# A decoder layer: order of the inner norms, of the first query's weights and of the compression's last weights

## The chip, the cores and the metric

The kernel runs on one core of one Trainium2 chip, as one program. The metric is device time in microseconds: 1134.9 us, the median of three runs from 1133.58 to 1134.92. Times inside the program come from one profiled execution.

## The reference

One decoder layer on 512 tokens of width 1024, all in float32. Two half-step SwiGLU FFNs (hidden width 2816) stand around a token mixer; each of the three is normed before and after:

```python
h = rms_norm(x, ffn1_pre[l])
x = x + 0.5 * rms_norm(swiglu(h, ffn1_w_gate[l], ffn1_w_up[l], ffn1_w_down[l]), ffn1_post[l])
h = rms_norm(x, mix_pre[l])
y = token_mixer(h, w_in[l], nsa_pe_k[l], nsa_w_ck1[l], nsa_w_ck2[l], nsa_pe_v[l],
                nsa_w_cv1[l], nsa_w_cv2[l], w_nsa_o[l], w_dil_o[l], w_mix_out[l])
x = x + rms_norm(y, mix_post[l])
h = rms_norm(x, ffn2_pre[l])
x = x + 0.5 * rms_norm(swiglu(h, ffn2_w_gate[l], ffn2_w_up[l], ffn2_w_down[l]), ffn2_post[l])
```

The mixer projects `h` with `w_in` and runs two kinds of attention side by side. The first, sparse attention (NSA), has 8 query heads in 2 groups and three branches: compressed keys and values (overlapping blocks of 32 tokens, through a hidden layer of 256 with gelu), selected blocks, and a window. At this length every block is selected, so that the second and third branch are both plain causal attention. The other kind, dilated attention, has 12 heads in 3 groups. Gates merge the two, and `w_mix_out` closes the mixer.

## The kernel before

Every float32 operand of a matrix product is split into two parts that TensorE takes: `hi`, a cast on ScalarE (line 107), and `lo`, the rest, a subtraction on VectorE (line 108); `split` does both. A product is then three matmuls, `mm3`, lines 130 to 132. Weights arrive in `raw`, three buffers of 1 MB that SyncE's queue fills, and their parts go to `whi` and `wlo`, three tiles of 128x1024 each. A buffer that rotates is free again when its last reader is done. Matrix results lie in eight PSUM banks under four names: S (3), T (2), V (1), F (2).

The code is traced in the order written; a scheduler then orders each engine's instructions by readiness, and every engine runs its own list in order, waiting on semaphores. `issue_after(x)` tells the scheduler that what is traced inside goes behind instruction `x` on the same engine; it adds no wait for `x` to end.

The work runs in this order: the first FFN's gate and up products (a Strassen form for most of the width), its down product (`ffn_down`, to about 349 us), the NSA part of the mixer (`nsa`, about 349 to 530), dilated attention (`dil`), the merge and `w_mix_out` (`mixer` and `down`, to about 800), and the second FFN.

**The norms between the parts.** A tile t holds 128 tokens. At the end of `ffn_down`, and of `down`, each tile takes these steps: mean square of the result (`meansq`, ScalarE, line 139), root (`rstd`: VectorE line 148, then a power on GpSimd, line 152), a multiplication by the gain, the update of x (lines 640 and 273), and, for the next part's norm, two more squares, another root, the scaled rows `tmp` (line 198), eight transposes (line 203), casts into `xh` (line 206) and rests into `xl` (line 210). `finish` starts the next norm and leaves the last three steps as a function in `self.pending`, to be called between later matmuls. In `ffn_down` the last product, T4, has two halves, for tiles 2 and 3; `between` runs after the first half. In `down`, the last eight weights of the second column half are held as split tiles, and each tile t runs through them (line 264).

**The start of the mixer.** `positions` transposes a small tile of position rows into a bank T (line 754). `nsa` projects the keys, in between calls the pending transposes, then projects the values (`v_nsa`, `v_weights`) and splits the first half of the key compression's weights (`hidden_early`, into x_s). Then 16 heads follow (four query pairs, two groups, two branches), with probabilities two heads behind the scores. For the first head: `proj_T` projects the query pair from a `raw` of its own, and `q_parts` writes the query's parts (lines 715 to 718, tiles Q). `hb_scores` multiplies with the keys (lines 724 and 725, banks S); line 730 adds the masked distances (`W`, the distance matrix `dm` times the head's slope, line 1050) and takes the maximum; line 731 is the exponential. `hb_probs` scales by the gate over the sum (ScalarE line 969, GpSimd line 971), transposes (line 980) and splits into PT; `hb_values` multiplies with the values (line 995). Between the heads stand the compression: `hidden` (line 814), first for the keys and then for the values, with its last two weight blocks split through `whi` and `wlo`; `gelu`, `compressed`, the compressed scores `cmp_pair` (line 916); and, as filling, units of the merge gates (`merge_unit`: a projection into a bank F, a copy, line 1085). Tiles NN, three of 128x1024, hold token sums in the first FFN and later rows of the second FFN's down weights (`mixer_sums`).

Of the kernel before, what the change touches and what calls it, by code (L numbers as in the profile page):

```python
# [26 lines left out]
DFF = 2816  # L27
NF = DFF // P
MIX_TAIL = 8
BUSY = 4, 2, 5, 2, 4  # L30
GATES_AHEAD = 4
LAG = 2
# [28 lines left out]
class Layer:  # L61
# [166 lines left out]
    def down(self, acts, wload, nk, tail, tags, post, finish):  # L228

        nc = self.nc
        gain = None
        self.pending = []
        ms0, y0 = [], []
        for d in range(2):
            banks = [self.bank(tag) for tag in ("STFV", "STFS")[d]]
            held = []

            def mm(t, k, w):  # L240
                c = slice(t * P, (t + 1) * P)
                hi, lo = acts[k]
                self.mm3(banks[t], hi[:, c], lo[:, c], w[0], w[1], k == 0, k == nk - 1)

            for k0 in range(0, nk, 2):
                src = wload(d, k0)
                if d == 1 and k0 >= nk - tail:
                    for j in range(2):
                        w = [self.slot(tags.pop(0), F32R) for _ in range(2)]
                        self.split(w[0], w[1], src[:, j])  # L250
                        held.append((k0 + j, w))
                else:
                    hi, lo = self.wsplit(src, [2, S])
                    for j in range(2):
                        for t in range(NT):
                            mm(t, k0 + j, (hi[:, j], lo[:, j]))
            if d == 0:
                gain = post()
                for t in range(NT):
                    ms0.append(self.meansq(banks[t], S))  # L260
                    nc.vector.tensor_mul(banks[t], banks[t], gain[0][0])
                    y0.append(banks[t])
                continue
            for t in range(NT):
                for k, w in held:
                    mm(t, k, w)
                if t in (1, 2) and self.pending:
                    self.pending.pop(0)()
                r = self.rstd([ms0[t], self.meansq(banks[t], S)])
                y1 = self.slot("ring")  # L270
                nc.vector.tensor_mul(y1, banks[t], gain[0][1])
                for x, y in ((self.x[2 * t], y0[t]), (self.x[2 * t + 1], y1)):
                    nc.vector.scalar_tensor_tensor(x, y, r, x, op0=OP.mult, op1=OP.add)
                finish(t, gain[1])
# [244 lines left out]
    def ffn_down(self, E, X, Y, wd, post, finish, xsrc):  # L519
# [132 lines left out]

        def between():
            scaled(2, 0, c[0])
            while self.pending:
                self.pending.pop(0)()

        product(half(parts["O"], 256), "T4", c, False, True, None, NP - EARLY, list(HOLD_TAGS), between,
                [(xh[:, k], xl[:, k]) for k in range(EARLY)])
        if gain[1] is None:  # L660
            update(2, (c[0], c22[0]))
            finish(2, None)
            r = self.rstd([self.meansq(c[1], S, 2.0), ms[3, 1]], 2.0)
            nc.vector.tensor_mul(c[1], c[1], gain[0][0])
            update(3, (c[1], c22[1]), r)
            finish(3, None)
        else:
            scaled(3, 0, c[1])
            for t in range(2):
                update(2 + t, (c[t], c22[t]))  # L670
            for t in range(2):
                finish(2 + t, gain[1])


    def wcols(self, segs):
# [36 lines left out]
    def q_parts(self, b, perm):  # L712
        nc = self.nc
        q0, q1 = self.slot("Q", F32R), self.slot("Q", F32R)
        nc.scalar.mul(q0[0:64], perm(b[0:64]), 0.125)
        nc.scalar.mul(q1[64:128], perm(b[64:128]), 0.125)
        nc.vector.scalar_tensor_tensor(q0[64:128], perm(b[0:64]), 0.125, q0[0:64].bitcast(F32), op0=OP.mult, op1=OP.subtract)
        nc.vector.scalar_tensor_tensor(q1[0:64], perm(b[64:128]), 0.125, q1[64:128].bitcast(F32), op0=OP.mult, op1=OP.subtract)
        return q0, q1
# [28 lines left out]
    def positions(self):  # L748
# [1 line left out]
        pe = self.slot("SP")  # L750
        nc.sync.dma_start(pe[0:16, 0:P], self.a["nsa_pe_k"][0].rearrange("(j r) d -> j (r d)", r=2))
        nc.sync.dma_start(pe[16:32, 0:P], self.a["nsa_pe_v"][0].rearrange("(j r) d -> j (r d)", r=2))
        b = self.bank("T")
        nc.tensor.transpose(b[:, 0:32], pe[0:32, 0:P], self.ident[0:32, 0:32])
        self.pe = self.sbt("pe", [P, 2, 16])
        nc.vector.tensor_copy(self.pe, b[:, 0:32].rearrange("p (a j) -> p a j", a=2))
# [42 lines left out]
    def hidden(self, which, gs, early):  # L799
# [6 lines left out]
        for u in range(4):  # L806
            if u < 2:
                w = early[4 * u:4 * u + 4]
            else:
                hi, lo = self.wsplit(r[:, 4 * u - 8:4 * u - 4], [4, 256])  # L810
                w = [(hi[:, i], lo[:, i]) for i in range(4)]
            for i in range(4):
                for j in range(2):
# [192 lines left out]
    def nsa(self, fillers):  # L1006
# [19 lines left out]
        kparts.append(self.k_parts(kw, ident))  # L1026
        gs.append(self.blocks(1, rows[1]))
        self.v_nsa(vw)
        early = self.hidden_early(0)
        self.oh, self.ol = [], []  # L1030
        heads = [(i, half, br) for i in range(4) for half in range(2) for br in range(2)]
# [2 lines left out]
        for n in range(len(heads) + LAG):  # L1034
            if n < len(heads) and n % 4 == 0:
                i = n // 4
                b, _ = self.proj_T(self.wcols([(i * 64, 64), (256 + i * 64, 64)]))
                qs[i] = self.q_parts(b, ident)
                if i:
                    cmps[i] = self.cmp_pair(i, qs[i])  # L1040
# [4 lines left out]
            if n < len(heads):  # L1045
                i, half, br = heads[n]
                h = i + 4 * half
                if br == 0:
                    ws[h] = self.slot("W")
                    nc.vector.tensor_scalar(ws[h], self.dm, -(2.0 ** -(h + 1)), None, op0=OP.mult)  # L1050
                kb, ka = kparts[br]
                live[n] = self.hb_scores(qs[i][half], ka[half], kb, half, ws[h])
            if m >= 0:
# [490 lines left out]
```

## Time and profile before

| | |
|---|---|
| median of three runs | 1134.9 us |
| the profiled execution | 1134.76 us |
| its span on the chip | 1133.0 us |
| TensorE busy (matmuls) | 1118.8 us |
| VectorE busy | 906.7 us |
| ScalarE busy | 638.2 us |
| GpSimd busy | 77.1 us |
| TensorE's granted clock, mean | 0.999 |

How to read the rows that follow: a row of a timeline has its start in us from the span's start, its length, the engine, the line of the code, the operation, output<-inputs and the count; in brackets the idle time of the engine before it and what ended that. PE is TensorE's matmul, PEld its weight load, DVE VectorE, ACT ScalarE, POOL GpSimd, SP SyncE. Matmuls are pipelined, so one matmul's length overlaps the next one's start. Rows of waits give the waiter, whom it waited for, the sum, the number and the longest. Rows of the chain, the work that ended last, have start, length, engine, output and line.

### The profile page before, as it was taken

What the parts mean: (1) busy time and instruction counts of PE and PEld (TensorE: products, weight loads), DVE (VectorE), ACT (ScalarE), POOL (GpSimd) and SP (SyncE); (2) the same over time, 40 slices, a digit from 0 to 9 for tenths busy, and PEclk for the clock granted to TensorE, in tenths of its full rate; (3) what the DMA queues carried; (4) which work ended last, traced back from release to release, by engine and by line L of the source; (5) the groups of instructions that cost most, each with busy time, mean ns of one, the idle gap of its engine ahead of it and who ended that gap; (6) DMA issues with size and microseconds to landing.
All of it is one profiled execution on the core that took longest, in us unless ns stands there. A gap on an engine that the chain in (4) does not pass through costs nothing.

```text
span 1133.0 us, 18466 instructions
## 1 busy us (share of the span) xinstructions
PE 1118.8 (99%) x6926; PEld 1001.4 (88%) x6926; DVE 906.7 (80%) x1563; ACT 638.2 (56%) x1145; POOL 77.1 (7%) x112
## 2 busy tenths in 40 slices
PE   9999999999999999999999999999999999999997
PEld 8889999998888987778888998788989999998886
DVE  6989999878676889687666687986878888979774
ACT  5435555566563788677565635644445555557562
POOL 1000000000011033243000000001000000000000
PEclk9999999999999999999999999999999999999999
DMA  9996665588763642211477759683233424357862
GB/s 321 331 301 201 188 197 186 154 276 285 262 208 85 187 120 85 62 38 50 146 245 242 235 177 300 201 295 114 66 121 122 131 88 127 122 169 239 287 224 84
DMA packets 152908, 206.01 MB, mean 182 GB/s; under 512 B 19794, under 2 KB 97906, under 8 KB 152564
## 3 DMA queue, kind: packets, MB, share of 16 engines
q1 hardware_dynamic: 152816, 204.85, 55.9%
q8 instruction: 54, 0.88, 0.3%
q14 instruction: 34, 0.28, 0.1%
q10 hardware_dynamic: 4, 0.00, 0.0%
HBM read 165.45 MB, written 39.37 MB: 181 GB/s over the span
## 4 chain that ended last, share of the span: by engine, by line
PE 90%; DVE 5%; ACT 2%; issue 1%; POOL 1%; DMA 1%; SPq 0%; POOLq 0%; DVEq 0%; ACTq 0%
PE pb_F L132 11%; PE pb_F L130 11%; PE pb_F L131 11%; PE pb_S L132 8%; PE pb_S L131 8%; PE pb_S L130 8%; PE pb_T L130 6%; PE pb_T L131 6%; PE pb_T L132 6%; PE pb_V L131 3%; PE pb_V L130 3%; PE pb_V L132 3%; PE pb_V L995 2%; PE pb_T L980 1%; DVE SP_s L730 1%
## 5 line engine op out<-in xcount | busy, mean ns | idle before, releaser
L107 ACT CAST whi<-raw 128x1024 fp32r<-128x1024 f32 (+1 forms) x215 | 219.9, 1023 | 249.2 <-issue 68.2
L108 DVE TENSOR_TENSOR wlo<-raw,whi 128x1024 fp32r<-128x1024 f32 (+1 forms) x215 | 255.0, 1188 | 96.5 <-ACT whi L107 92.2
L130 PE MATMUL pb_F<-xh_t,whi 128*128 128x512 f32 (+1 forms) x392 | 142.8, 364 | 0.4 <-ACT whi L107 0.4
L132 PE MATMUL pb_F<-xh_t,wlo 128*128 128x512 f32 (+1 forms) x392 | 141.6, 361 | 0.5 <-DVE wlo L108 0.5
L131 PE MATMUL pb_F<-xl_t,whi 128*128 128x512 f32 (+1 forms) x392 | 141.9, 362 | 0.0
L107 ACT CAST whi<-tmp_t 128x1024 fp32r<-128x1024 f32 x51 | 53.5, 1048 | 60.0 <-PE pb_S L131 22.0
L132 PEld LDWEIGHTS pb_F<-xh_t,wlo 128*128 128x128 f32 x392 | 74.1, 189 | 10.9 <-DVE wlo L108 1.0
L130 PEld LDWEIGHTS pb_F<-xh_t,whi 128*128 128x128 f32 x392 | 74.1, 189 | 10.4 <-ACT whi L107 0.6
L131 PEld LDWEIGHTS pb_F<-xl_t,whi 128*128 128x128 f32 x392 | 74.2, 189 | 9.5
L108 DVE TENSOR_TENSOR wlo<-tmp_t,whi 128x1024 fp32r<-128x1024 f32 x51 | 62.4, 1223 | 25.2 <-ACT whi L107 23.9
L130 PE MATMUL pb_S<-xh_t,whi 128*128 128x256 f32 (+1 forms) x240 | 73.2, 305 | 0.0
L132 PE MATMUL pb_S<-xh_t,wlo 128*128 128x256 f32 (+1 forms) x240 | 73.0, 304 | 0.0
L131 PE MATMUL pb_S<-xl_t,whi 128*128 128x256 f32 (+1 forms) x240 | 73.0, 304 | 0.0
L131 PE MATMUL pb_T<-xl_t,whi 128*128 128x256 f32 (+1 forms) x184 | 53.9, 293 | 0.0
L130 PE MATMUL pb_T<-xh_t,whi 128*128 128x256 f32 (+1 forms) x184 | 53.9, 293 | 0.0
L152 POOL TENSOR_TENSOR rs_t<-rs_t,mhalf_t 128x1 f32<-128x1 f32 x24 | 16.8, 701 | 543.3 <-DVE rs_t L148 543.2
L132 PE MATMUL pb_T<-xh_t,wlo 128*128 128x256 f32 (+1 forms) x184 | 53.8, 292 | 0.0
L971 POOL TENSOR_SCALAR SP_s<-SP_s,st_t 128x384 f32<-128x384 f32 (+2 forms) x48 | 45.8, 969 | 107.2 <-DVE st_t L907 78.1
L131 PEld LDWEIGHTS pb_S<-xl_t,whi 128*128 128x128 f32 x240 | 45.9, 191 | 1.9
L130 PEld LDWEIGHTS pb_S<-xh_t,whi 128*128 128x128 f32 x240 | 45.9, 191 | 1.9
L132 PEld LDWEIGHTS pb_S<-xh_t,wlo 128*128 128x128 f32 x240 | 45.9, 191 | 1.9
L108 DVE TENSOR_TENSOR PT_s<-pb_T,PT_s 128x512 fp32r<-128x512 f32 (+1 forms) x72 | 39.2, 559 | 6.3 <-ACT PT_s L107 5.6
(822 smaller groups left out, 3364.5 us busy)
## 6 DMA issues: line engine op xcount, KB each, us to landing
raw<-in_ffn_w_up_dram SPq DMA_DIRECT2D x36, 512.0 KB, 5.5
raw<-in_w_in_dram SPq DMA_DIRECT2D x18, 1024.0 KB, 5.5
raw<-in_ffn_w_gate_dram SPq DMA_DIRECT2D x35, 512.0 KB, 4.9
raw<-in_ffn_w_down_dram SPq DMA_DIRECT2D x14, 1024.0 KB, 5.7
raw<-tdram SPq DMA_DIRECT2D x14, 1024.0 KB, 5.5
NN_s<-in_ffn_w_down_dram SPq DMA_DIRECT2D x22, 512.0 KB, 5.2
tdram<-NN_s SPq DMA_DIRECT2D x22, 512.0 KB, 3.9
raw<-in_ffn_w_down_dram SPq DMA_DIRECT2D x6, 768.0 KB, 6.1
```

The costliest lines, as they stand in the source:

```text
L107: self.last_cast = self.nc.scalar.copy(dsthi, src).ins
L108: self.last_rest = self.nc.vector.tensor_sub(dstlo, src, dsthi.bitcast(F32)).ins
L130: mm(out, lhi, rhi, start=start, stop=False, skip_group_check=skip)
L131: mm(out, lhi, rlo, start=False, stop=False, skip_group_check=skip)
L132: mm(out, llo, rhi, start=False, stop=stop, skip_group_check=skip)
L152: nc.gpsimd.tensor_tensor(out=r, in0=v, in1=self.mhalf, op=OP.pow)
L730: nc.vector.tensor_tensor_reduce(p, s, w, -1.0, FLOOR, OP.add, OP.min, st_m)
L971: nc.gpsimd.tensor_scalar(pp, pp, st[:, 1, t:t + 1], None, op0=OP.mult)
L980: nc.tensor.transpose(b[:, o + (t - kk) * P:o + (t - kk + 1) * P], pt[pn][:, po + kk * P:po + (kk + 1) * P], self.ident)
L995: self.nc.tensor.matmul(out[:, kk * P:S], v, pp, start=first and kk == 0 and pi == 0, stop=False, skip_group_check=True)
```

## The change

In words:

- In `ffn_down`, `between` (after T4's half for tile 2) takes tile 2's root ahead of the pending transposes, and then updates x and starts the norm of tile 2 there. Before, tiles 2 and 3 were both updated after T4. This holds for both FFNs, with and without a next norm.
- In `down`, the pending transposes of a tile are called inside the loop over held weights, ahead of the fourth one, of tiles 2 and 3. Before, they were called behind all the held matmuls of tiles 1 and 2.
- `positions` transposes into bank V instead of T.
- The first query pair's weights are loaded and split ahead of `hidden_early`, into two NN tiles, and no longer through `whi` and `wlo`.
- In `hidden`, the last two weight blocks are queued behind the second query part on ScalarE (`last_q`, line 716), so behind the query's parts.
- Line 1050 (1057 after), the distances times slope, is queued behind the last rest, `last_rest`, on VectorE.

```diff
+POP = 3
...
-                for k, w in held:
+                for n, (k, w) in enumerate(held):
+                    if n == POP and t >= 2 and self.pending:
+                        self.pending.pop(0)()
                     mm(t, k, w)
-                if t in (1, 2) and self.pending:
-                    self.pending.pop(0)()
...
         def between():
             scaled(2, 0, c[0])
+            r = self.rstd([ms[2, 0], ms[2, 1]], 2.0)
             while self.pending:
                 self.pending.pop(0)()
+            update(2, (c[0], c22[0]), r)
+            finish(2, gain[1])
...
         if gain[1] is None:
-            update(2, (c[0], c22[0]))
-            finish(2, None)
...
             scaled(3, 0, c[1])
-            for t in range(2):
-                update(2 + t, (c[t], c22[t]))
-            for t in range(2):
-                finish(2 + t, gain[1])
+            update(3, (c[1], c22[1]))
+            finish(3, gain[1])
...
-        nc.scalar.mul(q1[64:128], perm(b[64:128]), 0.125)
+        self.last_q = nc.scalar.mul(q1[64:128], perm(b[64:128]), 0.125).ins
...
-        b = self.bank("T")
+        b = self.bank("V")
...
-                hi, lo = self.wsplit(r[:, 4 * u - 8:4 * u - 4], [4, 256])
+                with self.tc.issue_after(self.last_q):
+                    hi, lo = self.wsplit(r[:, 4 * u - 8:4 * u - 4], [4, 256])
...
         self.v_nsa(vw)
+        first = [self.slot("NN", F32R, (P, D)).rearrange("p (k f) -> p k f", k=KT) for _ in range(2)]
+        self.split(*first, self.wcols([(0, 64), (256, 64)]))
         early = self.hidden_early(0)
...
-                b, _ = self.proj_T(self.wcols([(i * 64, 64), (256 + i * 64, 64)]))
+                if i == 0:
+                    b, _ = self.proj_T(None, w=self.ktiles(first))
+                else:
+                    b, _ = self.proj_T(self.wcols([(i * 64, 64), (256 + i * 64, 64)]))
...
-                    nc.vector.tensor_scalar(ws[h], self.dm, -(2.0 ** -(h + 1)), None, op0=OP.mult)
+                    with self.tc.issue_after(self.last_rest):
+                        nc.vector.tensor_scalar(ws[h], self.dm, -(2.0 ** -(h + 1)), None, op0=OP.mult)
```

What the scheduler makes of it, at three places. Lines of the code after are one to seven higher than before.

VectorE at the first query, before. In numbered names, `raw_4375` holds the query's weights and `raw_4439` the compression's last ones:

```order
L108 TENSOR_TENSOR x_s_4372<-raw_4357,x_s_4371 128x512
L896 TENSOR_TENSOR V_s_4322<-pb_T_4297,V_s_4322 128x4x64
L108 TENSOR_TENSOR wlo_4379<-raw_4375,whi_4378 128x1024
L108 TENSOR_TENSOR wlo_4458<-raw_4439,whi_4457 128x1024
L896 TENSOR_TENSOR V_s_4351<-pb_T_4326,V_s_4351 128x4x64
L108 TENSOR_TENSOR wlo_4470<-raw_4439,whi_4469 128x1024
L899 TENSOR_SCALAR gate_t_4238<-gate_t_4238 128x96
L900 RECIPROCAL gate_t_4238<-gate_t_4238 128x96
L717 SCALAR_TENSOR_TENSOR Q_s_4407<-pb_F_4382,Q_s_4407 64x512
L718 SCALAR_TENSOR_TENSOR Q_s_4408<-pb_F_4382,Q_s_4408 64x512
L108 TENSOR_TENSOR x_s_4484<-raw_4481,x_s_4483 128x512
L730 ISA SP_s_4416,st_t_4415<-pb_S_4419,W_s_4413 128x512
```

VectorE at the same place after, from the query's parts on (the query's rest, into `NN_s_4358` from `raw_4359`, stands eleven rows above the first of these, and the first distances times slope, L1057, four rows above):

```order
L717 SCALAR_TENSOR_TENSOR Q_s_4407<-pb_F_4382,Q_s_4407 64x512
L718 SCALAR_TENSOR_TENSOR Q_s_4408<-pb_F_4382,Q_s_4408 64x512
L730 ISA SP_s_4416,st_t_4415<-pb_S_4419,W_s_4413 128x512
L730 ISA st_t_4415 128x1
L109 TENSOR_TENSOR wlo_4458<-raw_4439,whi_4457 128x1024
L730 ISA SP_s_4417,st_t_4415<-pb_S_4424,W_s_4413 128x384
L730 ISA st_t_4415 128x1
L730 ISA SP_s_4417,st_t_4415<-pb_S_4424,W_s_4413 128x128
L730 ISA st_t_4415 128x1
L730 ISA SP_s_4418,st_t_4415<-pb_S_4433,W_s_4413 128x256
L730 ISA st_t_4415 128x1
L109 TENSOR_TENSOR wlo_4470<-raw_4439,whi_4469 128x1024
```

The query's rest has moved up among the x_s rests, the compression's two last rests have moved behind the query's parts, between the first head's maxima (the L730 rows; each has a second one that reads the result).

ScalarE among the heads of the third query pair, before (PT are the probabilities' casts, CP the compressed ones', L731 the exponentials):

```order
L107 CAST CP_s<-pb_T 64x512
L107 CAST PT_s<-pb_T 128x512
L731 ACTIVATE SP_s,st_t<-SP_s,st_t 128x384
L731 ACTIVATE SP_s,st_t<-SP_s,st_t 128x128
L1085 COPY ring_s<-pb_F 128x512
L107 CAST PT_s<-pb_T 128x512
L731 ACTIVATE SP_s,st_t<-SP_s,st_t 128x256
L107 CAST PT_s<-pb_T 128x256
L731 ACTIVATE SP_s,st_t<-SP_s,st_t 128x512
```

ScalarE at the same place after:

```order
L108 CAST CP_s<-pb_T 64x512
L108 CAST PT_s<-pb_T 128x512 x2
L108 CAST PT_s<-pb_T 128x256
L731 ACTIVATE SP_s,st_t<-SP_s,st_t 128x512
L731 ACTIVATE SP_s,st_t<-SP_s,st_t 128x384
L731 ACTIVATE SP_s,st_t<-SP_s,st_t 128x128
L731 ACTIVATE SP_s,st_t<-SP_s,st_t 128x256
L108 CAST PT_s<-pb_T 128x512
L731 ACTIVATE SP_s,st_t<-SP_s,st_t 128x512
L108 CAST PT_s<-pb_T 128x512
```

One head's three casts of PT now stand together, and the exponentials of the next head come behind them instead of between them; the following head's casts are still mixed with them.

VectorE at the norms into the second FFN, tiles 1 and 2, before (`pb_T` is tile 1's transposed rows in the L210 rows and tile 1's result elsewhere; `pb_F` is tile 2's result):

```order
L198 SCALAR_TENSOR_TENSOR tmp_t<-x_s,rs_t,CP_s 128x512 x2
L148 TENSOR_SCALAR rs_t<-ss_t 128x1
L271 TENSOR_TENSOR ring_s<-pb_F,CP_s 128x512
L210 TENSOR_TENSOR xl_t<-pb_T,xh_t 128x4x128 x2
L273 SCALAR_TENSOR_TENSOR x_s<-pb_F,rs_t,x_s 128x512
L273 SCALAR_TENSOR_TENSOR x_s<-ring_s,rs_t,x_s 128x512
L108 TENSOR_TENSOR SP_s<-raw,SP_s 128x512 x2
```

And after:

```order
L272 TENSOR_TENSOR ring_s<-pb_F,CP_s 128x512
L274 SCALAR_TENSOR_TENSOR x_s<-pb_F,rs_t,x_s 128x512
L274 SCALAR_TENSOR_TENSOR x_s<-ring_s,rs_t,x_s 128x512
L109 TENSOR_TENSOR SP_s<-raw,SP_s 128x512
L211 TENSOR_TENSOR xl_t<-pb_T,xh_t 128x4x128
L149 TENSOR_SCALAR rs_t<-ss_t 128x1
L199 SCALAR_TENSOR_TENSOR tmp_t<-x_s,rs_t,CP_s 128x512 x2
L211 TENSOR_TENSOR xl_t<-pb_T,xh_t 128x4x128
L109 TENSOR_TENSOR SP_s<-raw,SP_s 128x512
```

The two rests of tile 1 no longer stand together ahead of tile 2's update: one stands behind it, the other behind tile 2's scaled rows (L199).

On SyncE, the load of the first merge unit's weights keeps its place behind the value compression's two loads, but its buffer is now freed by the last of the moved rests, and two loads into NN stand ahead of it. In the last FFN the order of the instructions is the same before and after on VectorE and ScalarE.

## The prediction

> **What bounds the kernel now.** I read the page first, then busy time in chosen windows, then waits, chain and timeline where TensorE stands still.
>
> ```profile
> span 1133.0 us, 18466 instructions
> PE 1118.8 (99%) x6926; PEld 1001.4 (88%) x6926; DVE 906.7 (80%) x1563; ACT 638.2 (56%) x1145; POOL 77.1 (7%) x112
> PE 90%; DVE 5%; ACT 2%; issue 1%; POOL 1%; DMA 1%; SPq 0%; POOLq 0%; DVEq 0%; ACTq 0%
> ```
>
> TensorE works nearly without a break, and the change leaves every matmul in place. So it can win only where TensorE waits, and lose only by adding waits. The profiled execution took 1134.76 us, 1.76 more than its span; the median of the runs is 1134.9. I count against 1134.76.
>
> Busy time by window (length; busy and instructions of PE, weight loads, DVE, ACT, POOL; clock; DMA), for the places that the change touches:
>
> ```profile
> 349.00:362.00 13.00, 11.67 (x95) 11.15 (x95) 9.39 (x20) 5.54 (x14) 2.90 (x8) 1.00 0.33 105
> 388.00:395.00 7.00, 6.07 (x28) 4.55 (x26) 4.70 (x6) 3.14 (x5) 0.00 (x0) 1.00 0.94 304
> 395.00:413.00 18.00, 17.78 (x111) 15.62 (x110) 15.93 (x41) 15.47 (x36) 2.99 (x3) 1.00 0.51 145
> 422.00:460.00 38.00, 37.30 (x212) 30.05 (x212) 34.71 (x109) 31.50 (x79) 15.79 (x16) 1.00 0.20 63
> 774.00:803.00 29.00, 28.60 (x170) 24.64 (x170) 21.34 (x39) 13.75 (x34) 4.41 (x8) 1.00 0.41 143
> ```
>
> Idle TensorE shows at 349 (the norm into the mixer) and at 388 (the first query's weights). From 395 to 460, the compression and the first heads, TensorE is full but VectorE is 34.71 of 38 us busy as well: there TensorE waits briefly and often, and a VectorE microsecond moved in is felt.
>
> **The change part by part.**
>
> (a) *Transpose of the position rows into bank V instead of T.* Waits of 340 to 362 (waiter <- releaser: us, times, longest):
>
> ```profile
> PE pb_T L754 <- DVE x_s L640: 1.2, 1, 1.2
> PEld pb_S L203 <- DVE tmp_t L198: 0.5, 2, 0.3
> ```
>
> The transpose waits 1.2 us until the residual update has read the second half's tile 2 out of bank T. Bank V's last reader is an update at 337.75 (next rows), 12 us before that one, so the wait goes whole: −1.2, and next in line is the first key projection, whose inputs are ready. Nothing new can be late there, so the end on the other side is 0.
>
> (b) *Norm of tile 2 begun inside the product.* The rows of VectorE, then TensorE:
>
> ```profile
> 337.75 0.74 DVE L640 SCALAR_TENSOR_TENSOR x_s<-pb_V,rs_t,x_s 128x512 f32<-128x512 f32 x1
> 349.48 0.75 DVE L640 SCALAR_TENSOR_TENSOR x_s<-pb_T,rs_t,x_s 128x512 f32<-128x512 f32 x1 [0.44 <-POOL rs_t L152]
> 355.75 1.42 DVE L198 SCALAR_TENSOR_TENSOR tmp_t<-x_s,rs_t,CP_s 128x512 f32<-128x512 f32 x2 [0.44 <-POOL rs_t L152]
> 356.56 1.32 PE L203 MATMUL pb_S<-ident_t,tmp_t 128*128 128x128 f32 x8
> ```
>
> From the update at 349.48 to the scaled rows at 355.75 pass 6.3 us, because tile 3's multiply, update and two scalings of the distances stand in between. They leave that path, so the rows are ready about 3 us sooner while TensorE arrives only 1.2 sooner. The two short weight-load waits (0.5 together) go. Tile 3 gives up its place for it: its chain ends where it did, and TensorE is earlier. I take −0.3, between −0.5 and +0.5.
>
> (c) *The first query's weights in two wide tiles, split before the compression's.* Waits of 385 to 412, then ACT, DVE and PE rows:
>
> ```profile
> PE pb_F L132 <- DVE wlo L108: 0.5, 1, 0.5
> PE pb_F L130 <- ACT whi L107: 0.4, 1, 0.4
> 381.95 1.14 ACT L107 CAST x_s<-raw 128x512 fp32r<-128x512 f32 x2
> 387.74 1.99 ACT L107 CAST whi<-raw 128x1024 fp32r<-128x1024 f32 x2
> 388.81 2.36 DVE L108 TENSOR_TENSOR wlo<-raw,whi 128x1024 fp32r<-128x1024 f32 x2 [1.25 <-ACT whi L107]
> 391.43 1.22 DVE L108 TENSOR_TENSOR wlo<-raw,whi 128x1024 fp32r<-128x1024 f32 x1
> ```
>
> The cast now stands where the first x_s cast stood, at 381.95; it takes about 1.0 and the rest 1.2, so both parts exist by about 385, 3 us before the projection wants them. −0.9, that is 0.5 + 0.4; no less than 0. So the query projection ends about 2.4 us earlier.
>
> (d) *The compression's last weights behind the query's parts.* Two rests of 1.2 us (half of 2.36, and 1.22) and two casts of 1.0 leave the time before the projection's end, where VectorE stood idle 3.1 us anyway, and enter the stage behind it.
>
> ```profile
> 395.23 2.08 PE L814 MATMUL pb_V<-x_s,PT_s 128*128 128x256 f32 x16
> 396.65 0.69 DVE L717 SCALAR_TENSOR_TENSOR Q_s<-pb_F,Q_s 64x512 fp32r<-64x512 f32 x1 [3.10 <-ACT Q_s L716]
> 397.37 0.69 DVE L718 SCALAR_TENSOR_TENSOR Q_s<-pb_F,Q_s 64x512 fp32r<-64x512 f32 x1
> 398.82 0.69 DVE L730 CUSTOM_DVE_ANT_0 SP_s<-pb_S,W_s 128x512 f32<-128x512 f32 x1
> 400.47 0.69 DVE L108 TENSOR_TENSOR x_s<-raw,x_s 128x512 fp32r<-128x512 f32 x1
> 408.52 0.23 PE pb_F L131
> 413.08 0.89 PE pb_T L980 x8
> ```
>
> I walk it from the projection's end E (395.2 now). VectorE: query parts done at E+2.9, the first masked maximum (L730) E+3.6, first rest E+4.8, the head's other three maxima (all four take from 398.82 to 400.47 now) E+5.9, second rest E+7.0. TensorE: 16 hidden matmuls to E+2, the first head's scores and the next head's first to E+4.2, so it waits 0.6 for the first rest; 8 matmuls of 0.12 and six score matmuls later it waits about 0.5 for the second. The four value-side rests (x_s) now start at E+7.0 instead of E+2.9, and each holds a quarter of the next 16 hidden matmuls. What follows is late by up to the whole 2.4. Against it, about five projection matmuls of 0.23, 1.1 us, now stand ahead of work that they stood behind. Net +1.3; ends 0 and +2.4.
>
> With (d) goes the row of distances times slope: it is now queued behind the last rest. The two that ran in idle time near 352 become one, and seven instead of six fall among the heads.
>
> ```profile
> L1050 DVE TENSOR_SCALAR W_s<-dm_t x8: 417/422/629, 352.2 to 490.7; 128x512 f32<-128x512 f32 x8
> 408.20 2.99 POOL L971 TENSOR_SCALAR SP_s<-SP_s,st_t 128x384 f32<-128x384 f32 x3 [50.22 <-DVE st_t L907]
> 410.31 0.63 DVE L1050 TENSOR_SCALAR W_s<-dm_t 128x512 f32<-128x512 f32 x1
> L971 POOL TENSOR_SCALAR SP_s<-SP_s,st_t 128x384 f32<-128x384 f32 x16 | 20.9, 1304 | 107.2 <-DVE st_t L907 78.1 <-DVE cden_t L906 15.9 <-PE pb_T L980 8.3
> ```
>
> Beside GpSimd's scaling it took 0.63, otherwise 0.42. I take +0.2, between +0.1 and the 1.3 of a whole GpSimd instruction (last row). The Trainium skill, SBUF — State Buffer, "Who interferes with whom", speaks against this: a tensor_scalar in a two-port mode and a GpSimd instruction lock each other out whole. By that rule one scaling more could stand through a GpSimd instruction of 1304 ns, and the total would be 1.1 higher, 1133.2. The 0.63 row, with GpSimd busy from before to after it, shows 0.2 of delay; here the trace speaks against the full lock.
>
> (e) *The heads.* The same condition puts each pair of heads' scaling, and all that hangs on it, behind the last rest of the probabilities PT. The casts of PT then run together instead of between the exponentials. Weight-load waits of 400 to 530:
>
> ```profile
> PEld pb_V L995 <- ACT PT_s L107: 3.8, 12, 0.7
> PEld pb_T L980 <- DVE PT_s L108: 1.8, 6, 0.4
> PEld pb_V L995 <- DVE PT_s L108: 1.1, 5, 0.3
> ```
>
> The values' matmuls wait for PT, 3.8 us in 12 waits for the cast. I let half of the first row go, 1.9, and give back 0.4 for scores that now come later: −1.5. Ends: −6.7 (all three rows), and +4 (second rival). This is my softest term.
>
> (f) *Norms into the second FFN: transposes of a tile three held weights into the product two tiles on.*
>
> ```profile
> PE pb_S L203 <- DVE tmp_t L198: 0.4, 1, 0.4
> 793.47 1.42 DVE L198 SCALAR_TENSOR_TENSOR tmp_t<-x_s,rs_t,CP_s 128x512 f32<-128x512 f32 x2 [0.73 <-POOL rs_t L152]
> 795.74 0.75 DVE L273 SCALAR_TENSOR_TENSOR x_s<-pb_V,rs_t,x_s 128x512 f32<-128x512 f32 x1
> ```
>
> This wait goes: nine held matmuls of 0.23, 2 us, now stand ahead of the transposes. But one half of tile 1's rest is queued behind tile 2's scaling (793.47), and the second FFN's first product needs it; tile 3's update (795.74) starts no sooner, and the last transposes hang on it. −0.3, between −0.8 and +1.0. In the last FFN the same code moves no instruction: 0.
>
> Sum: −1.2 −0.3 −0.9 +1.3 +0.2 −1.5 −0.3 = −2.7, so 1132.1.
>
> **The rivals.**
>
> *The heads gain nothing.* VectorE is 91% busy from 422 to 460; a different order does not shorten its work, and PT may wait as before. Without (e): 1134.76 −1.2 = 1133.6; if (d) costs its full 2.4, 1134.7. That is no measurable change, and the busy row speaks for it.
>
> *The heads run short of lead: slower.* Before, scores of later heads are taken early, between projections; now a pair's maxima start only when the pair two back has split its last PT. GpSimd's three scalings (2.99) must then end before the transposes, without a stock of finished heads. If six later pairs each bare one wait of 0.7, the longest in the rows above, that is +4.2: 1133.6 + 4.2 = 1137.8. It decides once the heads cost over 1.2 in all. The moved rests add to it, because they also hold a load:
>
> ```profile
> 392.67 14.00 SPq L682 DMA_DIRECT2D raw<-in_w_in_dram  x4
> raw<-in_w_in_dram SPq DMA_DIRECT2D x2, 1024.0 KB, 6.5
> ```
>
> The first merge unit's weights load at 392.67, when the last compression rest frees their buffer. That is now E+7.0, with 6.5 to landing E+13.5, and the cast comes at about E+13. SyncE's queue also meets the loads into NN earlier: those wait for the query projection, and the merge load stands behind them.
>
> *The heads gain all.* The three rows of (e) vanish, 6.7 instead of 1.5: 1126.9; half of that beyond the forecast gives 1129.5.
>
> *The added scaling stands still.* As said under (d), one more scaling held for a whole GpSimd instruction on VectorE's busy path: 1132.1 + 1.1 = 1133.2; the 0.63 row speaks against it.
>
> *The change does nothing.* For (a) to (c) this can't be: the waits have another cause only if the row names the wrong releaser, and the order of the three engines agrees with the rows.
>
> **How the numbers follow.** As summed, 1131 to 1132.6: 0.33. Heads gain all or most: 0.15. The scaling stands still: 0.05. No gain from the heads: 0.30. Short of lead: 0.17. A measurement of this kernel can tell about 0.2% from no change, 2.3 us, so faster is below 1132.6. The forecast and the large gain lie there: faster 0.48. The next two are no change that can be told: same 0.35. Slower 0.17. The range leaves 0.1 at each end: down to 1128.5, and up to 1136.5, where half of the slow case is still inside. Gains alone would give 1129 to 1134.5.
>
> **What would show it.** Where the compressed scores stand now:
>
> ```profile
> L916 PE MATMUL pb_S<-kcs_t,Q_s x32: 192/277/298, 421.6 to 499.0; 128*128 128x64 f32 x32
> ```
>
> (a) right: no wait of the position transpose. (c) right: the first query projection runs through, ending near 392.8. (d) right: new waits of 0.5 to 0.6 of L814 for wlo within 7 us behind it, the first probabilities' transposes near 413 as now, and the compressed scores only 1.1 us sooner than 421.6. (e) right: waits of L995 for the cast of PT below 2.5 us in sum, and the last head 2 us or more earlier; wrong: waits of L980 for GpSimd. (f) right: no wait at the first norm transposes, and one new short wait in the FFN's first product for xl. If the first heads are early by 2 us and the gain is gone by 530, the second or third case held and not mine.

## The result and the profile after

The changed kernel takes 1142.04 us (median of five runs, 1141.56 to 1143.86), where the kernel before takes 1134.9. The ratio on record is 1.0072, 95% interval 1.0061 to 1.0084 (these two medians alone give 1.0063; in the later sessions the kernel before had medians of 1133.9 to 1134.1). It is slower by about 8 us; the prediction was 1132.1, with 1128.5 to 1136.5 as its range. The profiled execution took 1143.05, 1.75 more than its span.

The page after, its first lines and the chain that ended last by engine:

```profile
span 1141.3 us, 18461 instructions
PE 1121.7 (98%) x6926; PEld 1003.7 (88%) x6926; DVE 909.8 (80%) x1563; ACT 636.8 (56%) x1145; POOL 80.0 (7%) x112
PE 86%; ACT 5%; DVE 4%; issue 2%; POOL 1%; DMA 1%; SPq 0%; POOLq 0%; DVEq 0%; ACTq 0%
```

The same matmuls (6926) are now busy 2.9 us longer, and TensorE stands 5.4 us more. Both numbers matter. Busy time by window shows where (columns as in the prediction: length, then busy and instructions of PE, weight loads, DVE, ACT, POOL, then clock and DMA):

```profile
349.00:362.00 13.00, 12.90 (x106) 12.46 (x107) 9.64 (x18) 6.09 (x15) 1.92 (x4) 1.00 0.32 104
388.00:395.00 7.00, 6.91 (x39) 5.88 (x38) 2.44 (x5) 2.75 (x5) 0.00 (x0) 1.00 0.79 261
395.00:413.00 18.00, 16.86 (x104) 14.44 (x102) 16.40 (x40) 15.44 (x34) 4.30 (x5) 1.00 0.59 177
422.00:460.00 38.00, 35.09 (x183) 28.16 (x183) 28.59 (x80) 24.28 (x56) 11.29 (x12) 0.96 0.31 98
520.00:550.00 30.00, 26.90 (x140) 21.84 (x140) 20.49 (x55) 20.15 (x46) 13.26 (x16) 0.94 0.26 80
```

At 349 and 388 TensorE has nearly closed its gaps (12.90 of 13 and 6.91 of 7 us). In the other three it does less than before, and in the last two the granted clock is below full, which no window of before was. The waits of 385 to 412:

```profile
PEld pb_V L815 <- DVE wlo L109: 1.6, 3, 0.8
PE pb_V L815 <- DVE wlo L109: 0.6, 2, 0.4
```

And of 400 to 560:

```profile
PEld pb_V L996 <- ACT PT_s L108: 5.8, 19, 0.5
PEld pb_T L981 <- POOL SP_s L972: 8.4, 9, 1.9
PE pb_T L981 <- POOL SP_s L972: 6.3, 8, 1.6
```

The last two rows were not there before: the transposes of the probabilities wait for GpSimd's scaling. The compressed scores and the rows of distances, and a fixed point behind the heads, the scaling of the distances for dilated attention, before and after:

```profile
L917 PE MATMUL pb_S<-kcs_t,Q_s x32: 193/277/297, 421.3 to 503.2; 128*128 128x64 f32 x32
L1057 DVE TENSOR_SCALAR W_s<-dm_t x8: 416/418/435, 387.1 to 526.7; 128x512 f32<-128x512 f32 x8
```

```profile
L1113 DVE TENSOR_SCALAR W_s<-dm_t x4: 221/221/222, 558.6 to 559.0; 128x128 f32<-128x128 f32 x4
```

```profile
L1120 DVE TENSOR_SCALAR W_s<-dm_t x4: 221/222/224, 568.2 to 568.6; 128x128 f32<-128x128 f32 x4
```

At the first compressed scores the changed kernel is 0.3 ahead (421.3 against 421.6), behind the heads 9.6 late. So about 10 us go between, among the heads. There are eight waits in four places; here is one of them, the first head of the third query pair, in rows of VectorE, GpSimd and TensorE after:

```profile
481.01 1.02 DVE L109 TENSOR_TENSOR PT_s<-pb_T,PT_s 128x512 fp32r<-128x512 f32 x2 [0.69 <-ACT PT_s L108]
481.95 0.42 DVE L1057 TENSOR_SCALAR W_s<-dm_t 128x512 f32<-128x512 f32 x1
482.51 0.69 DVE L730 CUSTOM_DVE_ANT_0 SP_s<-pb_S,W_s 128x512 f32<-128x512 f32 x1
487.84 0.16 DVE L908 TENSOR_TENSOR st_t<-st_t,gate_t 128x4 f32<-128x4 f32 x1
488.19 3.95 POOL L972 TENSOR_SCALAR SP_s<-SP_s,st_t 128x384 f32<-128x384 f32 x4 [13.87 <-ACT PT_s L108]
490.07 0.33 PE L981 MATMUL pb_T<-ident_t,SP_s 128*128 128x128 f32 x1 [0.49 <-POOL SP_s L972]
490.97 0.98 PE L981 MATMUL pb_T<-ident_t,SP_s 128*128 128x128 f32 x7 [0.57 <-POOL SP_s L972]
```

Before, the same head's first maximum, its scaling and its first transposes:

```profile
470.66 0.68 DVE L730 CUSTOM_DVE_ANT_0 SP_s<-pb_S,W_s 128x512 f32<-128x512 f32 x1
475.02 2.72 POOL L971 TENSOR_SCALAR SP_s<-SP_s,st_t 128x384 f32<-128x384 f32 x3 [15.52 <-DVE cden_t L906]
486.30 0.60 PE L980 MATMUL pb_T<-ident_t,SP_s 128*128 128x128 f32 x4
```

Read it as one path: last rest of the probabilities two heads back, row of distances, four maxima, four exponentials, the gate over the sum (its last step, at 487.84, stood behind another rest of PT), three scalings on GpSimd one after the other, transposes. From the row of distances to the first transposes that is 490.07 − 481.95 = 8.1 us, and TensorE has less work than that in between. Before, the maximum came at 470.66 and GpSimd was done by 477.74, 8.6 us ahead of the head's transposes at 486.3.

The second part of the loss is the clock. Busy time in four stretches of 3.41 us, and in one that holds another of the four places:

```profile
452.79:456.20 3.41, 1.28 (x10) 0.95 (x8) 1.90 (x5) 2.56 (x6) 3.26 (x4) 1.00 0.25 82
456.20:459.61 3.41, 3.41 (x13) 2.93 (x12) 1.29 (x2) 1.07 (x2) 2.51 (x3) 0.50 0.00 0
534.71:538.12 3.41, 1.35 (x8) 0.70 (x7) 1.77 (x7) 1.30 (x2) 3.37 (x4) 1.00 0.96 303
538.12:541.53 3.41, 3.41 (x14) 2.83 (x13) 1.38 (x2) 1.63 (x3) 2.34 (x3) 0.50 0.01 5
521.05:524.47 3.42, 2.37 (x14) 1.74 (x14) 1.76 (x5) 2.74 (x6) 3.27 (x5) 1.00 0.00 0
```

Behind two of the four places the clock is 0.50 for a stretch of 3.41 us, though TensorE is fully busy there: half of 3.41, so about 1.7 us lost each time, 3.4 in all in this execution. With TensorE's 6.3 us of waits for GpSimd that makes 9.7 of the 9.9 us (9.6 and the 0.3 that it was ahead).

### The profile page after: what moved, and what is told of

Its sections match the earlier page's. It is cut to its first block, busy times and chain, and to the rows that moved or that the text cites. A ratio compares the mean times of both kernels' runs of the same rounds, so it can differ in the third digit from the quotient of the medians.

```text
span 1141.3 us, 18461 instructions
## 1 busy us (share of the span) xinstructions
PE 1121.7 (98%) x6926; PEld 1003.7 (88%) x6926; DVE 909.8 (80%) x1563; ACT 636.8 (56%) x1145; POOL 80.0 (7%) x112
## 4 chain that ended last, share of the span: by engine, by line
PE 86%; ACT 5%; DVE 4%; issue 2%; POOL 1%; DMA 1%; SPq 0%; POOLq 0%; DVEq 0%; ACTq 0%
PE pb_F L131 11%; PE pb_F L133 10%; PE pb_F L132 10%; PE pb_S L131 8%; PE pb_S L133 8%; PE pb_S L132 8%; PE pb_T L131 6%; PE pb_T L132 6%; PE pb_T L133 6%; PE pb_V L131 3%; PE pb_V L133 3%; PE pb_V L132 3%; ACT SP_s L731 2%; PE pb_T L981 1%; PE pb_V L996 1%
## 5 line engine op out<-in xcount | busy, mean ns | idle before, releaser
L108 ACT CAST whi<-raw 128x1024 fp32r<-128x1024 f32 x214 | 218.9, 1023 | 244.6 <-issue 66.9
L109 DVE TENSOR_TENSOR wlo<-raw,whi 128x1024 fp32r<-128x1024 f32 x214 | 253.8, 1188 | 88.0 <-ACT whi L108 87.6
L131 PE MATMUL pb_F<-xh_t,whi 128*128 128x512 f32 (+1 forms) x384 | 139.8, 364 | 0.2 <-ACT whi L108 0.2
L132 PE MATMUL pb_F<-xl_t,whi 128*128 128x512 f32 (+1 forms) x384 | 138.9, 362 | 0.0
L972 POOL TENSOR_SCALAR SP_s<-SP_s,st_t 128x384 f32<-128x384 f32 (+2 forms) x48 | 48.6, 1031 | 123.3 <-DVE st_t L908 84.9
L108 ACT CAST PT_s<-pb_T 128x512 fp32r<-128x512 f32 (+1 forms) x72 | 33.3, 483 | 25.6 <-PE pb_T L981 15.6
```

Of the source, the lines that this page charges most:

```text
L108: self.last_cast = self.nc.scalar.copy(dsthi, src).ins
L109: self.last_rest = self.nc.vector.tensor_sub(dstlo, src, dsthi.bitcast(F32)).ins
L131: mm(out, lhi, rhi, start=start, stop=False, skip_group_check=skip)
L132: mm(out, lhi, rlo, start=False, stop=False, skip_group_check=skip)
L972: nc.gpsimd.tensor_scalar(pp, pp, st[:, 1, t:t + 1], None, op0=OP.mult)
```

## The experiments

**The condition on the row of distances, alone and left out.** The lead of a head is the time by which its scaled probabilities are ready before TensorE comes to their transposes. Theory 1: this condition alone takes the heads' lead. Theory 2: the moved compression rests make the heads late. To the kernel before is added

```diff
-                    nc.vector.tensor_scalar(ws[h], self.dm, -(2.0 ** -(h + 1)), None, op0=OP.mult)
+                    with self.tc.issue_after(self.last_rest):
+                        nc.vector.tensor_scalar(ws[h], self.dm, -(2.0 ** -(h + 1)), None, op0=OP.mult)
```

> The kernel before with one edit: the row of distances times slope is queued behind the last rest. Theory 1 (this condition alone takes the stock of finished heads away, so that TensorE waits for GpSimd's scaling at the transposes): about 10 us slower than before, 1143 to 1146, with TensorE's waits for GpSimd at the transposes of the probabilities 10 us or more, and the maxima of the later heads 8 to 17 us later than before. Theory 2 (the heads run late because the compression's last rests and the loads behind them moved): within 2 us of before. Theory 3 (both are needed): 1136 to 1139.

and the same lines are taken back from the changed kernel:

> The changed kernel without that condition, all other edits in place. Theory 1: the loss among the heads goes whole, and what is left is the sum of the other terms, 1132 to 1134; no wait for GpSimd at the transposes above 0.5 us. Theory 2: still 1139 or more. Theory 3: 1132 to 1134, so this run alone does not tell theory 1 from 3.

Measured: 1140.3 with the condition alone (ratio 1.0055, interval 1.0043 to 1.0068), and 1134.0 without it (0.9998, 0.9989 to 1.0007), beside 1134.0 for the kernel before. Waits of 400 to 560 with the condition alone:

```profile
PEld pb_T L980 <- POOL SP_s L971: 7.6, 9, 1.9
PE pb_T L980 <- POOL SP_s L971: 5.2, 8, 1.5
```

Theory 1 holds, theory 2 falls: the waits for GpSimd come with this one line, and without it one of 0.6 us is left to TensorE (at 413, the first head). Alone the line costs less than expected, 6.3 and not 9 to 12, but more than theory 3 gave it. In the changed kernel the line costs 8.0 (1142.0 − 1134.0). The condition alone makes the same four pairs of waits, 5.2 us where the changed kernel has 6.3, and in its profiled run the clock stays full in every microsecond of the heads, where the changed kernel loses 3.4.

**The other terms apart.** The changed kernel without the two conditions, `issue_after(self.last_rest)` at the distances and `issue_after(self.last_q)` in `hidden`:

> The changed kernel without that condition and without the compression's last weights behind the query's parts. By my term (d) it is 1.3 us faster than the kernel with them in place (the one without the condition on the distances alone), since the two waits of the compression for its rests go; by the profile after, where those waits grew, up to 2.5 us faster. If the hidden weights' place costs nothing, the two are equal.

And without the early split of the query's weights as well, so the norms and the position bank alone:

> The kernel before with the changes of the norms and the position bank alone: terms (a), (b) and (f), -1.8 in my sum, so about 1133; from the profile after, where the wait at the positions is gone and those at the norms are shorter, 1132.5 to 1133.5. The kernel without both conditions, which has the split of the first query's weights besides, should be 0.9 to 1.5 us faster than this one; if the query's weights were hidden anyway, equal.

Measured: 1133.91 (0.9999, 0.9990 to 1.0008) and 1132.61 (0.9988, 0.9979 to 0.9997). The norms and the bank gain 1.4 us, as expected. The early query weights then *cost* 1.3, against both expectations, and the condition in `hidden` on top of them nothing. Where the early weights cost is seen in rows of ScalarE and of TensorE, and in TensorE's waits of 400 to 560, of the kernel without the two conditions:

```profile
392.63 1.05 ACT L108 CAST whi<-raw 128x1024 fp32r<-128x1024 f32 x1 [2.40 <-DMA raw<-in_nsa_w_cv_dram]
393.58 0.59 ACT L715 ACTIVATE Q_s<-pb_F 64x512 fp32r<-64x512 f32 x1
```

```profile
395.70 0.50 PE L724 MATMUL pb_S<-KA_s,Q_s 128*128 128x512 f32 x1 [1.31 <-DVE Q_s L717]
```

```profile
PE pb_T L980 <- POOL SP_s L971: 1.5, 2, 1.0
```

The projection ends some 2 us sooner than in the norms-only kernel (392.36 against 394.33; 1.5 counted from the transpose of the positions, as this execution came there 0.5 earlier). But on ScalarE a cast of the value compression's weights now stands ahead of the query's parts and waits 2.40 us for its load, and on VectorE its rest stands ahead of line 717; TensorE then waits 1.31 for the query. The first head's transposes also stand earlier in TensorE's list (407.08 against 411.85) and wait 1.5 us for GpSimd. In the norms-only kernel, which has neither wait, that cast comes behind the query's parts. With the condition in `hidden` that cast is behind the query's parts, but so are the two rests of the *key* compression, which had their data all along. Windows of the norms-only kernel, then of the changed kernel without the condition on the distances:

```profile
388.00:395.00 7.00, 6.47 (x32) 5.13 (x32) 4.44 (x6) 2.69 (x6) 0.00 (x0) 1.00 1.03 343
395.00:413.00 18.00, 17.80 (x114) 15.68 (x113) 16.39 (x43) 15.90 (x36) 3.45 (x4) 1.00 0.47 126
```

```profile
388.00:395.00 7.00, 6.91 (x38) 5.88 (x37) 2.37 (x5) 2.84 (x5) 0.00 (x0) 1.00 0.79 252
395.00:413.00 18.00, 16.26 (x96) 13.56 (x94) 17.11 (x50) 15.47 (x40) 4.13 (x3) 1.00 0.59 175
```

Around the projection's end VectorE now works 2.37 of 7 us, where it worked 4.44, and behind it 17.11 of 18; TensorE gives up 1.5 us there (16.26 against 17.80).

**Splitting that condition.** Only the last of the two blocks stays behind the query's parts:

```diff
+                if u == 2:
+                    hi, lo = self.wsplit(r[:, 0:4], [4, 256])
+                else:
+                    with self.tc.issue_after(self.last_q):
+                        hi, lo = self.wsplit(r[:, 4:8], [4, 256])
```

> The changed kernel without the condition on the distances, and with only the last of the compression's two weight blocks queued behind the query's parts. If the loss of 1.4 us behind the query projection comes from rests that stand in VectorE's way there and from their waits, one of the two rests gone from there returns 0.6 to 1.2: 1132.8 to 1133.4. If the first heads are bound otherwise (GpSimd's scaling at 405 to 412), it stays at 1134.0.

Measured: 1134.53 (1.0003, 0.9994 to 1.0012): no gain. Then by compression, keys early and values behind the query's parts:

```diff
-                with self.tc.issue_after(self.last_q):
+                with self.tc.issue_after(self.last_q) if which else nullcontext():
                     hi, lo = self.wsplit(r[:, 4 * u - 8:4 * u - 4], [4, 256])
```

> The changed kernel without the condition on the distances, and with the query's parts ahead of the last weights of the value compression alone; those of the key compression stay early. The query projection ends 2 us earlier with its weights split early, but without the condition the query's parts stood behind a cast that waited 2.40 us for the value weights' load, and with it two rests of 1.2 us of the key compression came to stand in VectorE's full stretch behind the projection. This kernel avoids both: if those two are what eats the gain, it keeps 1 to 2 us of it, 1130.6 to 1131.8, and is the fastest of all. If the first heads are bound by VectorE whatever stands where, 1132.6 to 1134.

Measured: 1131.39 (0.9975, 0.9965 to 0.9985), 2.7 us faster than the kernel before and the fastest of all. Its windows:

```profile
388.00:395.00 7.00, 7.00 (x40) 6.07 (x38) 4.29 (x6) 3.38 (x9) 0.00 (x0) 1.00 1.09 357
395.00:413.00 18.00, 17.73 (x108) 14.99 (x107) 16.92 (x44) 15.87 (x36) 6.71 (x5) 1.00 0.62 176
```

TensorE is full in the first window and stands 0.3 us in the second, and VectorE works 4.29 us in the first. Beside the kernel without the two conditions only the place of the value compression's casts differs, and it is 2.5 us faster (1133.91 to 1131.39): both waits above are gone. So the early query weights are worth their gain if the casts that wait for a load stand behind the query's parts, and only those. Of the 1.5 us about 1.2 are kept (1132.6 to 1131.4). Why splitting by block failed was not followed to its end. There too the value side's cast stands behind the query's parts, by the scheduler's own choice, and one key rest does as well; TensorE's waits moved to the value side's first rests (1.8 us).

**Is it the lead?** The row of distances is queued behind an earlier rest: `ahead = self.last_rest`, taken ahead of `hb_probs`.

> The changed kernel, but the row of distances times slope is queued behind the last rest of the probabilities one head earlier (three heads back, not two). If the lead of the maxima over the transposes is what is short, a head's lead more, some 7 us, lets GpSimd end in time: the waits for GpSimd at the transposes fall from 14.7 us to below 4, no half clock is left, and the time is 1134 to 1137. If any such queueing on VectorE costs the time, whatever its lead, it stays above 1140.

Measured: 1141.88 (1.0063, 1.0050 to 1.0076), which by the expectation speaks against the lead. But the edit did not give it. VectorE in that kernel:

```profile
477.13 0.68 DVE L109 TENSOR_TENSOR CP_s<-pb_T,CP_s 64x512 fp32r<-64x512 f32 x1
477.85 0.69 DVE L109 TENSOR_TENSOR PT_s<-pb_T,PT_s 128x512 fp32r<-128x512 f32 x1
478.46 0.42 DVE L1058 TENSOR_SCALAR W_s<-dm_t 128x512 f32<-128x512 f32 x1
```

For the first head of a query pair the last rest traced was that of the same pair's compressed probabilities (CP), and so the row came only 3.5 us sooner (478.46 against 481.95). The run is inconclusive. With the rests of the probabilities kept in a list (`rests[-2]`), the row is queued three heads back as meant:

> The changed kernel, but each row of distances times slope is queued behind the last rest of the probabilities three heads back (kept in a list), not two; the first two rows have no such rest and go free. In the earlier run of that name's kind the anchor was whatever rest was traced last, for the first head of a query pair the compressed probabilities of the same pair, so it gave hardly more lead. If a head's lead is what is short (from a head's first maximum to its transposes 7.5 to 10 us are needed, and the heads with holes had 7.5 to 9.8), the holes at the transposes go: waits for GpSimd below 2 us, full clock, 1133.5 to 1135.5. If queueing the row behind any rest of the heads costs by itself, it stays above 1138.

Measured: 1136.08 (1.0017, 1.0008 to 1.0026). One wait is left of those of 400 to 560 for GpSimd, in two rows:

```profile
PEld pb_T L981 <- POOL SP_s L972: 0.7, 1, 0.7
PE pb_T L981 <- POOL SP_s L972: 0.4, 1, 0.4
```

The clock is full throughout. So a head's lead takes 6 of the 8 us away; 2 are left, a little more than expected (1133.5 to 1135.5). The weight loads of the values' matmuls wait 6.2 us for the cast of PT there, 3.7 in the kernel without the condition; that this is what is left is not shown.

**Is it GpSimd's part in the path?** ScalarE takes the widest of the three scalings:

```diff
-            if t == NT - 1:
+            if t >= NT - 2:
                 nc.scalar.mul(pp, pp, st[:, 1, t:t + 1])
```

> The changed kernel, but ScalarE and not GpSimd scales the third token tile's probabilities (384 wide), so that GpSimd scales two tiles of a head in place of three. If TensorE's holes at the transposes are the time of GpSimd's chain (2.99 us for three) that no lead covers any more, each of the four pairs of holes (2.5 or 1.5 us) shrinks by about the 1.3 us of the moved instruction: 5 us less, and with the half clock gone up to 8, so 1134 to 1138. If VectorE's late maxima alone set the holes, the scaling's engine doesn't matter: 1140 or more.

Measured: 1136.4 (1.0019, 1.0010 to 1.0028). TensorE's waits for GpSimd fall from 6.3 to

```profile
PE pb_T L981 <- POOL SP_s L972: 2.3, 5, 0.8
```

and the clock stays full. The waits are the tail of that path: either more lead or a shorter tail shortens them.

**What a hole costs.** A hole is a stretch in which TensorE stands. Into the kernel before, in the second FFN, eight holes:

```diff
+            if n and p > 2:
+                d = self.sbt("hole", [P, P])
+                nc.vector.tensor_copy(d, self.last_act[:, 0:P])
+                for _ in range(HOLES[p - 3]):
+                    nc.vector.tensor_scalar(d, d, 1.0, None, op0=OP.mult)
+                tr = nc.tensor.transpose(r11[:, 0:P], d, self.ident).ins
+                with self.tc.issue_after(tr):
```

> The kernel before, with eight holes of growing length put into TensorE's list in the second FFN (between its Strassen blocks, where the clock is full): a transposition that waits for a chain of 1 to 27 short VectorE operations on the block's result stands ahead of all matmuls of the next block. It tells what a hole costs beside its own length. Theory (a hole of about 2.5 us or more is followed by 3.4 us at half clock, as behind 453 and 535 in the profile after): the granted clock falls to 0.5 for some 3.4 us behind the longer holes, 1.7 us more each, and stays full behind those below 1.5 us. Rival (the two falls came from something else among the heads, such as what the other engines drew): full clock behind all eight.

> As the run with eight holes, but the chain starts from a product that is ready about 3 us earlier, and has 1 to 11 operations, so that the holes should be about 3 to 6 us, shorter than the 5.8 to 12.9 us of that run, behind each of which the clock fell. If the clock looks at fixed stretches of some 3.4 us (the falls and rises of that run lie on such a grid), some of the shortest holes leave it full, and every change of clock lies on the same grid. If any hole above 2.5 us brings a fall, all eight do.

Measured, one run each: 1226.26 and 1161.29. The first run's holes came out at 5.8 to 12.9 us, and the clock fell in all eight. Its first one, on stretches of 3.41 us:

```profile
859.15:862.56 3.41, 0.70 (x6) 0.49 (x5) 2.40 (x4) 1.54 (x2) 0.00 (x0) 1.00 0.59 176
862.56:865.97 3.41, 0.33 (x2) 0.33 (x3) 3.29 (x8) 0.40 (x1) 0.00 (x0) 0.50 0.61 208
865.97:869.39 3.42, 3.42 (x18) 3.42 (x18) 0.00 (x0) 0.00 (x0) 0.00 (x0) 0.50 0.00 0
```

The second run's were 0.24 to 1.38 us (five), 4.06, 5.00 and 6.74: the five left the clock full, the three brought it down. Around the 4.06 one:

```profile
964.61:968.03 3.42, 1.60 (x14) 1.40 (x12) 3.28 (x9) 1.95 (x3) 0.00 (x0) 1.00 0.36 78
968.03:971.44 3.41, 1.17 (x10) 1.20 (x11) 3.41 (x8) 0.41 (x1) 0.00 (x0) 1.00 0.89 306
971.44:974.85 3.41, 3.41 (x18) 3.41 (x17) 0.82 (x3) 0.08 (x1) 0.00 (x0) 0.50 0.00 0
```

The rival falls: a hole alone brings the clock down, with no attention head near. The first run is 92.4 us longer than the kernel before (1133.88 in that session), and its eight holes are 72.5 us long together; so each costs some 2.5 us beside its own length. None of these holes lies between 1.38 and 4.06, where the longest pairs of waits among the heads are (1.6 and 0.6); what decides there is below.

## Why the prediction was wrong

The step that failed is (e): "I let half of the first row go, 1.9, and give back 0.4 for scores that now come later: −1.5". That line costs 8.0 in its place. The row that I wanted halved grew, 3.8 to 5.8, and it grew as well where the lead was given back (6.2) or the tail cut short (7.4): no kernel with the condition shows the gain that (e) counted on. Why the weight loads wait longer for the casts was not tested. The rival "short of lead" named the mechanism, with GpSimd's scalings that "must then end before the transposes", and the mark that would show it. It was underrated twice. In chance: 0.17, although the order showed that the row of distances, and so a pair's maxima, would stand behind rests of two heads back. And in size: it was priced as six waits of 0.7 us, the longest wait that was in the trace. A wait that the trace does not show has no reason to be as long as those that it shows. The path could have been added up from rows of before: four maxima, four exponentials, GpSimd's 2.99 for three scalings and what stands between them, against the work that TensorE has between two heads' transposes. Then there is the half clock, 3.4 us, which no row of before could show.

Point by point:

- (a), (b), (f), the bank and the norms, −1.8: right, −1.4 measured for the three together. The wait of the position transposes is gone, and 349 to 362 is nearly full. The two short weight-load waits that (b) saw go are still there (0.5 in two, in the profile after).
- (c), the query's weights, −0.9: the projection does end sooner, but alone this costs +1.3. The step "both parts exist by about 385" was true (383.9) and not enough: I did not list what stands on ScalarE ahead of the query's parts without (d), a cast that waits for a load.
- (d), the compression's rests, +1.3: on top of (c) it measures 0. Its waits are there (1.6 us of weight loads in three, in the profile after), but it also frees the query from that cast, which I had not seen. (c) and (d) together cost +1.4, where the sum had +0.4.
- The added scaling, +0.2, with its rival of 1.1: none of the eight scalings took over 0.435 us. By the Trainium skill, SBUF — State Buffer, "Who interferes with whom", one could have stood behind a GpSimd instruction; the rows after hardly met one. Other runs' rows did: in the kernel with `ahead` a scaling at 453.78 took 0.68 and ended 0.29 behind the GpSimd scalings beside it (454.46 against 454.17), as if held until then, while the 0.63 row of before ended inside one (410.94 against 411.19). So the trace before spoke less clearly against the full lock than I took it to; the longest delay in any run, 0.26, is far from 1.1.
- The sum without (e) was 1133.6; without its line the changed kernel takes 1134.0. That they lie so close is partly luck: the changes were to win 1.2 and win nothing against the kernel before in the same session (1134.0), and the execution that I counted from lay 0.8 above that. (c) missed by 2.2 one way and (d) by 1.2 the other.

## What to carry to other kernels

An order that runs work ahead of its need is a stock, and a condition that ties a cheap instruction at the head of a long path (row, maximum, exponential, sum, scaling, transpose) to a late event empties it: add up the path from that instruction to the engine that must not wait, and compare it with the work in between, before looking at how long today's waits are. When a transfer or a split is moved ahead, list what now stands in each engine's queue ahead of the next urgent instruction: here a cast that waits for a load, ahead of the query's parts, cost more than the move won, and putting just the value compression's casts behind them gave the fastest kernel. A hole of some 2 us in TensorE's work can cost 1.7 us beside its own length, and holes of 5.8 to 12.9 us cost some 2.5 each.

## What the runs showed of the hardware

The granted clock fell and rose only at points of a fixed grid of 3.41 us: in the profile after it changes at 456.20, 459.61, 538.12 and 541.53, and 538.12 − 456.20 is 24 times 3.413. What counted, as far as these runs show, was the busy share of TensorE in such a stretch. Well below half, the next stretch ran at 0.50: shares of 0.38 and 0.40 (after), 0.34 (1.17 of 3.41, eight holes, second run). At 0.69 (521.05) and 0.60 (944.13, the same run with holes) it did not fall. Near half it went both ways: in the kernel with `ahead`,

```profile
449.20:452.61 3.41, 1.79 (x12) 1.55 (x13) 1.25 (x3) 2.31 (x5) 3.41 (x4) 1.00 0.09 26
486.75:490.16 3.41, 1.65 (x12) 1.39 (x12) 1.10 (x4) 2.12 (x5) 3.41 (x5) 1.00 0.00 0
490.16:493.57 3.41, 3.41 (x11) 2.73 (x10) 1.95 (x4) 1.26 (x3) 1.37 (x2) 0.50 0.00 0
```

0.48 (1.65 of 3.41) brought a fall, and 0.52 none; 0.47 (1.60 of 3.42 at 964.61, above) and 0.45 (1.53 of 3.42 at 705.91, without the two conditions) brought none either, so the edge isn't sharp in these modelled busy times. So the same pair of waits, some 2 us, would cost 2 or 3.7 us by where it falls on the grid, which is what I take for the difference between 8.0 and 6.3 for the same line; it was not tested by moving the grid alone. The five runs of the changed kernel fit: the three shortest (1141.56 to 1142.04) have a mean clock of 0.997, the next (1143.05) 0.996, the longest (1143.86) 0.995. The Trainium skill, TensorE: Matmul & The Clock Gate, "Part 1: The HAM clock gate", tells of a free-running window of 3413 ns at whose end the clock is halved or restored; the trace agrees with it. Its working rule there, no idle gap above some 3.4 us ("HAM oscillation"), is too generous for this kernel: some 2 us of waits within one stretch were enough (1.28 of 3.41 busy).
